# A state-space mixer's convolution, pace and sums, written in another way

## The chip, the cores and the metric

The kernel runs on one core of a Trainium2 chip. A core has engines that work side by side, each through its own row of instructions, in order: TensorE (PE) for matrix products, with the loading of weights (PEld) beside it; VectorE (DVE), ScalarE (ACT) and GpSimd (POOL) for everything else; SyncE (SP), which here only issues transfers (DMAs). Products are collected in PSUM, everything else lies in SBUF. The metric is the device time of one execution in microseconds (us). A profiled execution gives a trace of every instruction, with a clock granted to PE, where 1.00 is full speed.

## What is computed

One layer of a hybrid block on x of 1024 positions by 1024 channels, in float32. Two mixers read the same normalised input; each is mapped back to 1024 channels, gated and merged; a gated feed-forward layer follows. The change is in the second mixer, Mamba-2:

```python
def mamba2_mixer(z, xbc, dt, conv_w, conv_b, dt_bias, a_log, d_skip, w_norm):
    xbc = jax.nn.silu(causal_dwconv(xbc, conv_w, conv_b))      # 4 taps along the sequence
    xs, bm, cm = ...            # x: 4 groups x 8 heads x 64; B and C: 4 groups x 128
    delta = jax.nn.softplus(dt + dt_bias); a = -jnp.exp(a_log) * delta; xdt = xs * delta
    def step(state, inp):       # over chunks
        acum = jnp.cumsum(ac, axis=1)
        decay = jnp.exp(jnp.where(mask, acum_t - acum_s, -jnp.inf))
        y = einsum(C.B, decay, x) + einsum(C, state) * jnp.exp(acum)
        state = state * jnp.exp(a_last) + einsum(B, jnp.exp(a_last - acum), x)
        return state, y
    y = y + xs * d_skip
    y = y * jax.nn.silu(z)
    return rms_norm(y per group of 512 channels) * w_norm
...
merged = jax.nn.sigmoid(gate_a) * y_a + jax.nn.sigmoid(gate_b) * y_b
```

## The kernel before

**Dense products.** A projection has a block of 128 output channels as its unit (`Dense.unit`, L85): its weights (128x1024) are loaded, cast on ACT to a high part (`wh`, L75), and the low part is the difference (`wl`, L76, on GpSimd in this stage). For each half of the sequence (512 positions) 8 slices of the input are multiplied three times, low by high, high by low, high by high (L81, L82, L83): 24 products of 128x128 by 128x512 into one PSUM tile `dps` of a pool `psd` with three tiles. Then `evac` takes the tile away. With `fine=True` a unit yields after every three products, else only after each half.

**The fill.** `Fill.to(n)` draws steps of such units until n are done, so that dense products stand in PE's row between the smaller products of a recurrence. What is written between two calls of `fill.to` is the order in which instructions are issued; within it a scheduler may still set one engine's instructions some places apart, so PE's row is not quite the program's. The program's stages follow each other: front projections, the HGRN recurrence (up to about 828 us of the trace, with dense units, and the gate units GA7, GB0 and GB1, as its fill), `mamba_phase` (to about 1343 us), the branch products `dqs` whose operands `yr` are loaded from `ya_d` and `yb_d` (L946), and the feed-forward layer.

**The state-space stage.** It runs over 4 groups of 8 chunks of 128 positions. A group's six blocks (four of x, then B, then C) are units of the fill. Their `evac` (L797) copies the PSUM tile to `xp` in SBUF (L798), makes the fourth tap on ACT out of PSUM (L800), the other three on DVE out of `xp` at shifted columns (L802), and then Silu with `act`. `act` (L131) also loads ACT's table (L135) where the function belongs to another set than the last one: Exp and Ln share a set, Sigmoid and Silu have one each; the operation itself then has line L137.

For each chunk, `prepare` (L811) loads the decay rows `ac` and `eb`, makes them on ACT (L827, L137), transposes x (`trx`, L831), multiplies C by B (`cb`, L833), masks it (`cm`, L835), scales x twice (`xd`, `kx`, L837, L841), transposes B into the second half of the same PSUM tile (`cb`, L842), copies it out (`bt`, L844) and multiplies decay and `cm` (L845). `mix` (L850) has the products `yi` (within the chunk, L861), `yx` (from the state `Sm`, L867) and `sps` (into the state, L874), and adds them to x on DVE (last: L881). `finish` (L883) works on half a group, 512 positions: GpSimd multiplies z on (L890), ACT squares, DVE adds the four squares, `col_sums` splits the sum in two parts (`csh` on ACT, `csl` on DVE, L192) and PE sums over channels with two products into `smm` (L199, L200); Ln, Exp and a product (L901) norm the rows, and they are stored to `yb_d` (L902).

The order: 12 half units, `prepare(0, 0)`, then in every chunk the `prepare` of the next one, `finish` of the previous group's halves in chunks F0 = 1 and F1 = 4, the chunk's share of the fill at once (1.5 half units, or 5/8 of one in the last group), and `mix`. The last group's two `finish` calls stand after its last `mix`, then the LATE = 7 half units that are left.

Of the kernel before, what the change touches and what calls it, by code (L numbers as in the profile page):

```python
# [17 lines left out]
F0, F1 = 1, 4  # L18
LATE = 7
NGB = 2  # L20
# [101 lines left out]
def hybrid_block(ctx, tc, x, w_mod, w_ada, w_blk, w_i, w_ba, w_bb, w_o, w_g, w_u, w_d,  # L122
# [117 lines left out]
    def gate_evac(which, n):  # L240
        dst = (ga_d, gb_d)[which]

        def evac(th, ps):
            sg = wp.tile([P, TH], F32, tag="ge", name="ge")
            act(sg, ps, AF.Sigmoid)
            nc.sync.dma_start(out=dst[n, :, TH * th:TH * th + TH], in_=sg)
        return evac

    def gate_units(which, n0, n1, fine=False):
        for n in range(n0, n1):  # L250
            yield from dn.unit(w_blk[(B_GA, B_GB)[which] + n], uh, ul, gate_evac(which, n), fine=fine)
# [530 lines left out]
    def mamba_phase():  # L782
        with tc.tile_pool(name="m", bufs=2, reuse_waits="tile") as mp, \
                tc.tile_pool(name="mps", bufs=1, space=PSUM, reuse_waits="tile") as pp:
            grp, pre, state = {}, {}, {}

            def dense_x(g):
                xT = mp.tile([P, 4, T], F32, tag="xT", name="xTm", bufs=3)
                bT = mp.tile([P, T], F32, tag="bT", name="bT")
                cT = mp.tile([P, T], F32, tag="cT", name="cT")  # L790
                grp[g] = (xT, bT, cT)
                for blk, dst in [(4 * g + j, xT[:, j, :]) for j in range(4)] + [(16 + g, bT), (20 + g, cT)]:
                    xp = mp.tile([P, T + 3], F32, tag="xp", name="xp")
                    V.memset(xp[:, 0:3], 0.0)
                    cw = lambda j: cl[:, C_CW + 4 * blk + j:C_CW + 4 * blk + j + 1]

                    def evac(th, ps, xp=xp, dst=dst, cw=cw):  # L797
                        S.copy(xp[:, 3 + TH * th:3 + TH * th + TH], ps)  # L798
                        d = dst[:, TH * th:TH * th + TH]
                        S.activation(d, ps, AF.Identity, scale=cw(3))  # L800
                        for j in (2, 1, 0):
                            V.scalar_tensor_tensor(d, xp[:, TH * th + j:TH * th + j + TH], cw(j), d,  # L802
                                                   op0=ALU.mult, op1=ALU.add)
# [7 lines left out]
            def prepare(g, ch):  # L811
                xT, bT, cT = grp[g][:3]
                hs = slice(HG * g, HG * g + HG)
                cs = slice(P * ch, P * ch + P)
                h64 = lambda ap: ap.rearrange("p (h q) -> p h q", h=HG)
                ac = mp.tile([P, HG, P], F32, tag="ac", name="ac", bufs=2)
                nc.sync.dma_start(out=ac, in_=ac_d[ch, hs, :][None].broadcast_to([P, HG, P]))
                eb = None
                if ch:
                    eb = mp.tile([P, 4, P], F32, tag="eb", name="eb")  # L820
                    a2 = ac_d[ch, hs, :].rearrange("(j e) t -> e j t", e=2)
                    for e in range(2):
                        nc.sync.dma_start(out=eb[64 * e:64 * e + 64], in_=a2[e][None].broadcast_to([64, 4, P]))
                    act(eb, eb, AF.Exp)
                for h in range(HG):
                    n = HG * g + h
                    S.activation(ac[:, h, :], ac[:, h, :], AF.Relu, bias=acum[:, ch, n:n + 1], scale=-1.0)  # L827
                act(ac, ac, AF.Exp, scale=-1.0)
                tr = pp.tile([P, TH], F32, tag="tr", name="trx")
                for j in range(4):  # L830
                    PE.transpose(out=tr[:, P * j:P * j + P], in_=xT[:, j, cs], identity=ident)  # L831
                cb = pp.tile([P, TH], F32, tag="cb", name="cb")
                PE.matmul(cb[:, 0:P], bT[:, cs], cT[:, cs], start=True, stop=True)  # L833
                cm = mp.tile([P, P], F32, tag="cm", name="cm")
                V.tensor_tensor(cm, cb[:, 0:P], triu, op=ALU.mult)  # L835
                xd = mp.tile([P, TH], F32, tag="xd", name="xd")
                V.tensor_tensor(h64(xd), h64(tr), delta[:, ch, hs][:, :, None].broadcast_to([P, HG, HP]), op=ALU.mult)  # L837
                kx = bt = None
                if ch < TT - 1:
                    kx = mp.tile([P, TH], F32, tag="kx", name="kx")  # L840
                    V.tensor_tensor(h64(kx), h64(tr), wdec[:, ch, hs][:, :, None].broadcast_to([P, HG, HP]), op=ALU.mult)  # L841
                    PE.transpose(out=cb[:, P:2 * P], in_=bT[:, cs], identity=ident)  # L842
                    bt = mp.tile([P, P], F32, tag="bt", name="bt")
                    V.tensor_copy(bt, cb[:, P:2 * P])  # L844
# [3 lines left out]
                pre[g, ch] = (ac, eb, xd, kx, bt)  # L848

            def mix(g, ch):  # L850
                xT, bT, cT = grp[g][:3]
                hs = slice(HG * g, HG * g + HG)
                cs = slice(P * ch, P * ch + P)
                h64 = lambda ap: ap.rearrange("p (h q) -> p h q", h=HG)
                ac, eb, xd, kx, bt = pre.pop((g, ch))
                st = state.get(g)
                yi = pp.tile([P, 4, P], F32, tag="yi", name="yi")
# [5 lines left out]
                y = mp.tile([P, 4, P], F32, tag="yt", name="yt")  # L863
                if ch:
                    yx = pp.tile([P, 4, P], F32, tag="yx", name="yx")
                    for j in range(4):
                        PE.matmul(yx[:, j, :], st[:, P * j:P * j + P], cT[:, cs], start=True, stop=True)  # L867
                    V.tensor_tensor(y, yx, eb, op=ALU.mult)
                    V.tensor_tensor(y, y, yi, op=ALU.add)
                else:  # L870
                    V.tensor_copy(y, yi)
                if ch < TT - 1:
                    sps = pp.tile([P, TH], F32, tag="st", name="sps")
                    PE.matmul(sps, bt, kx, start=True, stop=True)  # L874
                    sn = state[g] = mp.tile([P, TH], F32, tag="S", name="Sm")
                    if ch:
                        V.tensor_tensor(h64(sn), h64(st), eal[:, ch, hs][:, :, None].broadcast_to([P, HG, HP]), op=ALU.mult)
                        V.tensor_tensor(sn, sn, sps, op=ALU.add)
                    else:
                        V.tensor_copy(sn, sps)  # L880
                V.tensor_tensor(xT[:, :, cs], xT[:, :, cs], y, op=ALU.add)  # L881

            def finish(g, hf):  # L883
                xT = grp[g][0]
                sl = slice(TH * hf, TH * hf + TH)
                sqs = mp.tile([P, TH], F32, tag="S", name="sqs")
                for j in range(4):
                    zs = mp.tile([P, TH], F32, tag="zs", name="zs", bufs=2)
                    nc.sync.dma_start(out=zs, in_=z_d[4 * g + j, :, sl])
                    G.tensor_tensor(xT[:, j, sl], xT[:, j, sl], zs, op=ALU.mult)  # L890
                    sq = sqs if j == 0 else mp.tile([P, TH], F32, tag="yt", name="sq")
# [3 lines left out]
                sm = pp.tile([P, TH], F32, tag="cb", name="smm")  # L895
                col_sums(sm, sqs, mp, ("yt", "yt"), V)
# [7 lines left out]
            fill = Fill(chain(*[dense_x(g) for g in range(GB)], gate_units(1, NGB, 8)))  # L904
            fill.to(12)
            prepare(0, 0)
            at = [12]
            for g in range(GB):
                n = 12 if g < GB - 1 else 16 - 2 * NGB - LATE
                at += [at[8 * g] + n * (c + 1) / 8 for c in range(TT)]  # L910
            for i in range(TT * GB):
                g, ch = divmod(i, TT)
                if i + 1 < TT * GB:
                    prepare(*divmod(i + 1, TT))
                if g and ch == F0:
                    finish(g - 1, 0)
                if g and ch == F1:
                    finish(g - 1, 1)
                fill.to(at[i + 1])
                mix(g, ch)  # L920
                if g == GB - 1 and ch == 7:
                    finish(g, 0)
                if g == GB - 1 and ch == 7:
                    finish(g, 1)
# [432 lines left out]
```

## Time and profile before

| | |
|---|---|
| runs, us | 2398.66, 2406.07, 2404.76 |
| median | 2404.76 |
| profiled execution | 2397.53, of which the span of the trace is 2395.7 |
| mean granted PE clock | 0.98 |
| state-space stage in the trace | about 828 to 1343 us |

Times in the trace are counted from the span's start. In a row of it, `PE L83 MATMUL dps<-uh,wh` is the instruction of line 83 on PE that writes `dps` from `uh` and `wh`; "L842 <- DVE cm L835" is idle time of PE ahead of its line 842 that DVE's `cm` of line 835 ended.

### The profile page before, as it was taken

What the parts mean: (1) busy time and instruction counts of PE and PEld (TensorE: products, weight loads), DVE (VectorE), ACT (ScalarE), POOL (GpSimd) and SP (SyncE); (2) the same over time, 40 slices, a digit from 0 to 9 for tenths busy, and PEclk for the clock granted to TensorE, in tenths of its full rate; (3) what the DMA queues carried; (4) which work ended last, traced back from release to release, by engine and by line L of the source; (5) the groups of instructions that cost most, each with busy time, mean ns of one, the idle gap of its engine ahead of it and who ended that gap; (6) DMA issues with size and microseconds to landing.
All of it is one profiled execution on the core that took longest, in us unless ns stands there. A gap on an engine that the chain in (4) does not pass through costs nothing.

```text
span 2395.7 us, 32127 instructions
## 1 busy us (share of the span) xinstructions
PE 2256.0 (94%) x12412; PEld 1824.6 (76%) x12412; DVE 1611.3 (67%) x2452; ACT 1096.7 (46%) x1894; POOL 393.8 (16%) x239
## 2 busy tenths in 40 slices
PE   7799999999999998989897999999999999999996
PEld 4578888877777786767675788888778888888785
DVE  6967655548788467787878434458887666655657
ACT  4533333046666658778787411223533333322232
POOL 0600000012222222222213000003410000013224
PEclk9999999999999999999999999999999999999999
DMA  7344325611111222333444734433233222244544
GB/s 272 103 148 132 128 90 194 196 40 54 59 54 54 93 67 93 122 108 118 135 126 158 254 129 154 135 102 129 76 122 106 92 71 88 78 151 145 167 150 152
DMA packets 116032, 290.23 MB, mean 121 GB/s; under 512 B 12324, under 2 KB 27172, under 8 KB 115880
## 3 DMA queue, kind: packets, MB, share of 16 engines
q1 hardware_dynamic: 115880, 288.19, 36.2%
q8 instruction: 97, 1.59, 0.3%
q14 instruction: 55, 0.45, 0.1%
HBM read 234.52 MB, written 53.62 MB: 120 GB/s over the span
## 4 chain that ended last, share of the span: by engine, by line
PE 65%; DVE 14%; ACT 7%; DMA 4%; issue 3%; POOL 2%; POOLq 0%; DVEq 0%; SPq 0%; ACTq 0%
PE fps L81 8%; PE fps L82 8%; PE fps L83 8%; PE dps L81 8%; PE dps L82 8%; PE dps L83 8%; PE dqs L81 4%; PE dqs L82 4%; PE dqs L83 4%; DVE xTm L802 2%; DMA ac<-ac_d 1%; PE hps L83 1%; PE hps L81 1%; PE hps L82 1%; ACT ac L827 1%
## 5 line engine op out<-in xcount | busy, mean ns | idle before, releaser
L81 PE MATMUL dps<-uh,wl 128*128 128x512 f32 x800 | 330.4, 413 | 7.3 <-POOL wl L76 3.8
L82 PE MATMUL dps<-ul,wh 128*128 128x512 f32 x800 | 320.9, 401 | 0.0
L83 PE MATMUL dps<-uh,wh 128*128 128x512 f32 x800 | 320.8, 401 | 0.0
L75 ACT CAST wh<-raw 128x1024 fp32r<-128x1024 f32 x113 | 118.4, 1049 | 266.9 <-PE fps L83 147.4
L76 POOL TENSOR_TENSOR wl<-raw,wh 128x1024 fp32r<-128x1024 f32 x50 | 131.8, 2638 | 552.0 <-ACT wh L75 460.8
L81 PEld LDWEIGHTS dps<-uh,wl 128*128 128x128 f32 x800 | 156.2, 195 | 38.2 <-issue 6.0
L83 PEld LDWEIGHTS dps<-uh,wh 128*128 128x128 f32 x800 | 153.7, 192 | 32.9 <-issue 0.8
L82 PEld LDWEIGHTS dps<-ul,wh 128*128 128x128 f32 x800 | 154.4, 193 | 29.6 <-issue 1.3
L1225 POOL TENSOR_TENSOR wdr<-wdr,rws 128x512 f32<-128x512 f32 x44 | 70.8, 1612 | 529.9 <-DMA rws<-g_d 368.7
L81 PE MATMUL dqs<-yp,wl 128*128 128x512 f32 x384 | 149.3, 390 | 1.1 <-ACT yp L191 1.1
L82 PE MATMUL dqs<-yp,wh 128*128 128x512 f32 x384 | 149.5, 390 | 0.0
L83 PE MATMUL dqs<-yp,wh 128*128 128x512 f32 x384 | 149.2, 389 | 0.0
L191 ACT CAST cw<-raw 128x512 fp32r<-128x512 f32 x131 | 80.7, 621 | 130.3 <-PE fps L83 87.1
L76 DVE TENSOR_TENSOR wl<-raw,wh 128x1024 fp32r<-128x1024 f32 x63 | 78.3, 1243 | 91.1 <-ACT wh L75 91.1
L81 PE MATMUL fps<-t,cw 128*128 128x512 f32 x352 | 137.0, 389 | 0.5 <-ACT p L1115 0.5
L82 PE MATMUL fps<-t,cw 128*128 128x512 f32 x352 | 136.9, 389 | 0.0
L83 PE MATMUL fps<-t,cw 128*128 128x512 f32 x352 | 136.9, 389 | 0.0
L81 PE MATMUL fps<-wd,wl 128*128 128x512 f32 x304 | 119.1, 392 | 3.1 <-DVE wl L76 3.1
L802 DVE SCALAR_TENSOR_TENSOR xTm<-xp,cl,xTm 128x512 f32<-128x512 f32 x96 | 101.9, 1072 | 27.7 <-ACT xTm L800 26.7
L82 PE MATMUL fps<-wd,wh 128*128 128x512 f32 x304 | 118.9, 391 | 0.0
L83 PE MATMUL fps<-wd,wh 128*128 128x512 f32 x304 | 118.7, 391 | 0.0
L192 DVE TENSOR_TENSOR cw<-raw,cw 128x512 fp32r<-128x512 f32 x109 | 79.7, 733 | 41.4 <-ACT cw L191 40.2
(364 smaller groups left out, 5635.1 us busy)
## 6 DMA issues: line engine op xcount, KB each, us to landing
raw<-in_w_blk_dram SPq DMA_DIRECT2D x78, 512.0 KB, 3.4
raw<-h_d SPq DMA_DIRECT2D x44, 512.0 KB, 3.5
wa<-in_w_ada_dram SPq DMA_DIRECT2D x32, 512.0 KB, 4.6
ac<-ac_d SPq DMA_DIRECT2D x32, 512.0 KB, 4.1
raw<-in_w_g_dram SPq DMA_DIRECT2D x26, 512.0 KB, 3.9
raw<-in_w_u_dram SPq DMA_DIRECT2D x26, 512.0 KB, 3.4
wdr<-in_w_d_dram SPq DMA_DIRECT2D x44, 256.0 KB, 3.1
h_d<-sg SPq DMA_DIRECT2D x18, 512.0 KB, 2.9
```

The costliest lines, as they stand in the source:

```text
L75: nc.scalar.copy(wh, raw)
L76: (eng or self.lo).tensor_tensor(wl, raw, wh.bitcast(F32), op=ALU.subtract)
L81: nc.tensor.matmul(ps, sl, mh, start=first, stop=False)
L82: nc.tensor.matmul(ps, sh, ml, start=False, stop=False)
L83: nc.tensor.matmul(ps, sh, mh, start=False, stop=last)
L191: S.copy(hi, src)
L192: eng.tensor_tensor(lo, src, hi.bitcast(F32), op=ALU.subtract)
L802: V.scalar_tensor_tensor(d, xp[:, TH * th + j:TH * th + j + TH], cw(j), d, op0=ALU.mult, op1=ALU.add)
L827: S.activation(ac[:, h, :], ac[:, h, :], AF.Relu, bias=acum[:, ch, n:n + 1], scale=-1.0)
L1225: G.tensor_tensor(raw, raw, g2r[:, halves[nh]], op=ALU.mult)
```

## The change

- **Convolution.** The copy to `xp` is gone. The three taps on DVE read the PSUM tile, each half by itself at 509 to 512 columns; six columns around the border between the halves are kept in a small tile `edge`, and the second half's first three columns get three small products more. Silu is applied after every second block, to both. B and C come first in a group, the x blocks behind them.
- **Fill.** All units in this stage yield after three products. A chunk's share (12 such steps; 6.5 in the last group) is drawn in two halves, one ahead of `mix` and one behind it, and LEAD = 12 steps more stand ahead of the first chunk; LATE is now 32 such steps.
- **Chunk.** `ac` is loaded two chunks ahead (three buffers), `eb` in `fetch_e`. Both `cb` products come right behind the transpositions. The product of decay and `cm` is a part of its own, `scores`, behind the `mix` before. `mix` has the order `yx`, `sps`, `yi`.
- **Sums.** `finish` is cut in `squares` (up to the split) in chunks 0 and 3 and `finish` (from the sums on) two chunks later; `smm` is a tile of `psd`. In the last group half 0 is squared in chunk 5, and half 1 after the last `mix`; eight steps of the fill stand ahead of the last `finish`.
- **Gates.** Gate units that run in fine steps, those in HGRN's fill too, have Exp, Ln, Exp for Sigmoid.

```diff
-F0, F1 = 1, 4
-LATE = 7
+F0, F1 = 0, 3
+LATE, LEAD = 32, 12
...
+            if logs:
+                act(sg, ps, AF.Exp, scale=-1.0)
+                act(sg, sg, AF.Ln, bias=ones[:, 0:1])
+                act(sg, sg, AF.Exp, scale=-1.0)
+            else:
+                act(sg, ps, AF.Sigmoid)
...
-                for blk, dst in [(4 * g + j, xT[:, j, :]) for j in range(4)] + [(16 + g, bT), (20 + g, cT)]:
-                    xp = mp.tile([P, T + 3], F32, tag="xp", name="xp")
-                    V.memset(xp[:, 0:3], 0.0)
+                held = []
+                for blk, dst in [(16 + g, bT), (20 + g, cT)] + [(4 * g + j, xT[:, j, :]) for j in range(4)]:
+                    held.append((blk, dst))
+                    edge = mp.tile([P, 6], F32, tag="edge", name="edge")
...
-                        S.copy(xp[:, 3 + TH * th:3 + TH * th + TH], ps)
                         d = dst[:, TH * th:TH * th + TH]
                         S.activation(d, ps, AF.Identity, scale=cw(3))
+                        if th:
+                            V.tensor_copy(edge[:, 3:6], ps[:, 0:3])
+                        else:
+                            V.tensor_copy(edge[:, 0:3], ps[:, TH - 3:TH])
                         for j in (2, 1, 0):
-                            V.scalar_tensor_tensor(d, xp[:, TH * th + j:TH * th + j + TH], cw(j), d,
+                            o = 3 if th else 3 - j
+                            V.scalar_tensor_tensor(d[:, o:], ps[:, o + j - 3:TH + j - 3], cw(j), d[:, o:],
                                                    op0=ALU.mult, op1=ALU.add)
-                        if blk >= 20:
-                            act(d, d, AF.Silu, bias=cl[:, C_CB + blk:C_CB + blk + 1])
-                        elif th:
-                            act(dst, dst, AF.Silu, bias=cl[:, C_CB + blk:C_CB + blk + 1])
-                    yield from dn.unit(w_blk[B_X + blk], uh, ul, evac)
+                            if th:
+                                V.scalar_tensor_tensor(d[:, 0:3], edge[:, j:j + 3], cw(j), d[:, 0:3],
+                                                       op0=ALU.mult, op1=ALU.add)
+                        if th and len(held) == 2:
+                            for k, t in held:
+                                act(t, t, AF.Silu, bias=cl[:, C_CB + k:C_CB + k + 1])
+                            held.clear()
+                    yield from dn.unit(w_blk[B_X + blk], uh, ul, evac, fine=True)
...
+                PE.matmul(cb[:, 0, :], bT[:, cs], cT[:, cs], start=True, stop=True)
+                if ch < TT - 1:
+                    PE.transpose(out=cb[:, 1, :], in_=bT[:, cs], identity=ident)
...
-                V.tensor_tensor(ac, ac, cm[:, None, :].broadcast_to([P, HG, P]), op=ALU.mult)
+            def scores(g, ch):
+                ac, cm = pre[g, ch][:2]
+                V.tensor_tensor(ac, ac, cm[:, None, :].broadcast_to([P, HG, P]), op=ALU.mult)
...
-            def finish(g, hf):
+            def squares(g, hf):
...
+                split(*hl, sqs, V)
+                fin[g, hf] = sqs, hl
+            def finish(g, hf):
...
+                sqs, (hi, lo) = fin.pop((g, hf))
+                sm = psd.tile([P, TH], F32, tag="d", name="smm")
+                PE.matmul(sm, ones_r, lo, start=True, stop=False)
+                PE.matmul(sm, ones_r, hi, start=False, stop=True)
...
             for i in range(N):
                 g, ch = divmod(i, TT)
+                if i + 2 < N:
+                    fetch(*divmod(i + 2, TT))
                 if i + 1 < N:
                     prepare(*divmod(i + 1, TT))
...
+                if g:
+                    for f, hf in ((F0, 0), (F1, 1)):
+                        if ch == f:
+                            squares(g - 1, hf)
+                        if ch == f + 2:
+                            finish(g - 1, hf)
...
+                fill.to((share(i) + share(i + 1)) / 2)
                 mix(g, ch)
...
+                if i + 2 < N:
+                    fetch_e(*divmod(i + 2, TT))
+                if i + 1 < N:
+                    scores(*divmod(i + 1, TT))
+                if g == GB - 1 and ch == 5:
+                    squares(g, 0)
+                fill.to(share(i + 1))
+            finish(g, 0)
+            squares(g, 1)
+            fill.to(total + 8)
+            finish(g, 1)
             fill.drain()
```

**PE, a chunk of the second group in which sums are made**, before (`dps` are the dense products, `uh` and `ul` the two parts of the input, `mk` the identity; the lone `cb` transposition of L842 stands at another place of the chunk, behind dense products):

```order
L83 MATMUL dps<-uh_93,wh 128x512
L861 MATMUL yi<-ac,xd 64x128 x8
L867 MATMUL yx<-cT,Sm 128x128 x4
L874 MATMUL sps<-kx,bt 128x512
L199 MATMUL smm<-csl,ones_r 128x512
L200 MATMUL smm<-csh,ones_r 128x512
L831 MATMUL trx<-mk,xTm 128x128 x4
L81 MATMUL dps<-uh_92,wl 128x512
L82 MATMUL dps<-ul_94,wh 128x512
L833 MATMUL cb<-cT,bT 128x128
L83 MATMUL dps<-uh_92,wh 128x512
```

and with the change, first at `prepare` and the sums, and 18 dense products later at `mix`:

```order
L83 MATMUL dps<-uh_92,wh 128x512
L850 MATMUL trx<-mk,xTm 128x128 x4
L852 MATMUL cb<-cT,bT 128x128
L854 MATMUL cb<-mk,bT 128x128
L936 MATMUL smm<-csl,ones_r 128x512
L937 MATMUL smm<-csh,ones_r 128x512
L81 MATMUL dps<-uh_92,wl 128x512
```

The rows of `mix`:

```order
L83 MATMUL dps<-uh_93,wh 128x512
L889 MATMUL yx<-cT,Sm 128x128 x4
L892 MATMUL sps<-kx,bt 128x512
L897 MATMUL yi<-ac,xd 64x128 x8
L81 MATMUL dps<-uh_93,wl 128x512
```

The sums stood right behind the mix whose group's half they close; now they stand behind `prepare`, with both `cb` products ahead of them, and there are dense products between `prepare` and `mix` and behind `mix`.

**ACT, at the end of the HGRN stage**, before (`sc` and `oT` belong to HGRN's last chunks, `ge` is a gate, `csh` the high part of a split sum, `wh` a weight's):

```order
L682 COPY sc<-sc_ps_3616 128x128
L719 ACTIVATE sq<-oT 128x512
L191 CAST csh<-sq 128x512
L137 ACTIVATE ge<-dps 128x512
L135 ACT_TABLE_LOAD
L137 ACTIVATE sq<-sum,kc 128x512
L75 CAST wh<-raw 128x1024
L137 ACTIVATE sq<-sq 128x512
L135 ACT_TABLE_LOAD
```

and with the change:

```order
L724 ACTIVATE sq<-oT 128x512
L191 CAST csh<-sq 128x512
L137 ACTIVATE ge<-dps 128x512
L75 CAST wh<-raw 128x1024
L137 ACTIVATE ge<-ge,mk 128x512
L137 ACTIVATE ge<-ge 128x512
L137 ACTIVATE sq<-sum,kc 128x512
L137 ACTIVATE sq<-sq 128x512
L135 ACT_TABLE_LOAD
L806 ACTIVATE bT<-dps,cl 128x512
```

The table load between the gate and `sum` is gone, two operations on `ge` are added, and the cast of the gate's weight stands ahead of the two operations on `sum`.

**SP, from the last loads of z to the first operand of the branch products**, before (`raw` is a weight of the branch products, `gb_d` the gates' store):

```order
L889 DMA zs<-z_d 128x512 x2
L902 DMA yb_d<-xTm 128x512 x4
L70 DMA raw<-in_w_ba_dram 128x1024
L902 DMA yb_d<-xTm 128x512 x4
L246 DMA gb_d<-ge 128x512 x2
L946 DMA yr<-ya_d 128x1024
```

and with the change:

```order
L943 DMA yb_d<-xTm 128x512 x4
L251 DMA gb_d<-ge 128x512
L922 DMA zs<-z_d 128x512
L943 DMA yb_d<-xTm 128x512 x4
L1008 DMA yr<-ya_d 128x1024 x2
```

The load `yr` stands behind the last stores to `yb_d` in both; between the stores of half 0 and those of half 1 there is now a load of z.

More of the change, by code (lines that the diff above doesn't have):

```diff
@@ L250, in gate_units @@
         for n in range(n0, n1):
-            yield from dn.unit(w_blk[(B_GA, B_GB)[which] + n], uh, ul, gate_evac(which, n), fine=fine)
+            yield from dn.unit(w_blk[(B_GA, B_GB)[which] + n], uh, ul, gate_evac(which, n, fine), fine=fine)
     def combo(pool, tag, src, eng=V, **k):
@@ L823, in prepare @@
                         nc.sync.dma_start(out=eb[64 * e:64 * e + 64], in_=a2[e][None].broadcast_to([64, 4, P]))
-                    act(eb, eb, AF.Exp)
+                    dec[g, ch, 1] = eb
+            h64 = lambda ap: ap.rearrange("p (h q) -> p h q", h=HG)
+            def prepare(g, ch):
+                xT, bT, cT = grp[g]
+                hs = slice(HG * g, HG * g + HG)
+                cs = slice(P * ch, P * ch + P)
+                tr = pp.tile([P, TH], F32, tag="tr", name="trx")
+                for j in range(4):
+                    PE.transpose(out=tr[:, P * j:P * j + P], in_=xT[:, j, cs], identity=ident)
+                cb = pp.tile([P, 2, P], F32, tag="cb", name="cb")
+                PE.matmul(cb[:, 0, :], bT[:, cs], cT[:, cs], start=True, stop=True)
+                if ch < TT - 1:
+                    PE.transpose(out=cb[:, 1, :], in_=bT[:, cs], identity=ident)
+                ac, eb = dec.pop((g, ch)), dec.pop((g, ch, 1), None)
                 for h in range(HG):
@@ L828, in prepare @@
                 act(ac, ac, AF.Exp, scale=-1.0)
[L829 to L833, printed above, removed]
+                if ch:
+                    act(eb, eb, AF.Exp)
                 cm = mp.tile([P, P], F32, tag="cm", name="cm")
-                V.tensor_tensor(cm, cb[:, 0:P], triu, op=ALU.mult)
+                V.tensor_tensor(cm, cb[:, 0, :], triu, op=ALU.mult)
                 xd = mp.tile([P, TH], F32, tag="xd", name="xd")
@@ L862, in mix @@
                                   start=True, stop=True)
[L863 removed]
+                y = mp.tile([P, 4, P], F32, tag="yt", bufs=1, name="yt")
                 if ch:
[L865 to L867 removed]
                     V.tensor_tensor(y, yx, eb, op=ALU.mult)
[L869 to L871 removed]
                 if ch < TT - 1:
[L873 to L874 removed]
                     sn = state[g] = mp.tile([P, TH], F32, tag="S", name="Sm")
@@ L880, in mix @@
                         V.tensor_copy(sn, sps)
+                if ch:
+                    V.tensor_tensor(y, y, yi, op=ALU.add)
+                else:
+                    V.tensor_copy(y, yi)
                 V.tensor_tensor(xT[:, :, cs], xT[:, :, cs], y, op=ALU.add)
-            def finish(g, hf):
+            def squares(g, hf):
                 xT = grp[g][0]
                 sl = slice(TH * hf, TH * hf + TH)
-                sqs = mp.tile([P, TH], F32, tag="S", name="sqs")
+                sqs = mp.tile([P, TH], F32, tag="sqs", name="sqs", bufs=1)
+                hl = [mp.tile([P, TH], F32R, tag="hl", name=n) for n in ("csh", "csl")]
                 for j in range(4):
@@ L902, in finish, with share @@
                     nc.sync.dma_start(out=yb_d[4 * g + j, :, sl], in_=xT[:, j, sl])
-            fill = Fill(chain(*[dense_x(g) for g in range(GB)], gate_units(1, NGB, 8)))
-            fill.to(12)
-            prepare(0, 0)
[L907 to L911, printed above, removed]
+            N = TT * GB
+            fill = Fill(chain(*[dense_x(g) for g in range(GB)], gate_units(1, NGB, 8, True)))
+            total = 96 * GB + 16 * (8 - NGB) - LATE
+            fetch(0, 0)
+            fill.to(96 + LEAD)
+            fetch(0, 1)
+            fetch_e(0, 1)
+            prepare(0, 0)
+            scores(0, 0)
+            def share(i):
+                if i <= N - TT:
+                    return 96 + LEAD + 12 * i
+                a = 96 + LEAD + 12 * (N - TT)
+                return a + (total - a) * (i - N + TT) / TT
+            for i in range(N):
                 g, ch = divmod(i, TT)
-                if i + 1 < TT * GB:
+                if i + 2 < N:
+                    fetch(*divmod(i + 2, TT))
+                if i + 1 < N:
                     prepare(*divmod(i + 1, TT))
[L915 to L919, printed above, removed]
-                mix(g, ch)
[L921 to L924, printed above, removed]
+                if g:
[5 more added lines that the diff above has]
+                fill.to((share(i) + share(i + 1)) / 2)
+                mix(g, ch)
+                if i + 2 < N:
+                    fetch_e(*divmod(i + 2, TT))
+                if i + 1 < N:
+                    scores(*divmod(i + 1, TT))
[6 more added lines that the diff above has]
+            finish(g, 1)
             fill.drain()
```

41 lines of the change are left out of this document (22 added, 19 removed).

## The prediction

> **What bounds the kernel now.** I read the page's busy times first, then its stretches by stage, then PE's waits in the state-space stage, then single rows. The two rows of the page:
>
> ```profile
> span 2395.7 us, 32127 instructions
> PE 2256.0 (94%) x12412; PEld 1824.6 (76%) x12412; DVE 1611.3 (67%) x2452; ACT 1096.7 (46%) x1894; POOL 393.8 (16%) x239
> ```
>
> PE is busy 94% of the span, so a change pays where PE stands, runs at a lower clock, or gets fewer products; it gets the same number here. The stretches of the stage (columns: stretch, its length, then busy us and instructions of PE, PEld, DVE, ACT, POOL, then PE's granted clock, DMA share and GB/s) are the lead into the first group, groups 0 to 3, and the tail:
>
> ```profile
> 828.00:893.00 65.00, 65.00 (x288) 53.81 (x287) 35.21 (x38) 31.41 (x54) 17.71 (x7) 1.00 0.29 88
> 893.00:1002.00 109.00, 99.78 (x569) 77.57 (x568) 87.24 (x124) 86.70 (x167) 21.41 (x11) 1.00 0.28 94
> 1002.00:1114.00 112.00, 100.53 (x551) 78.36 (x550) 89.58 (x135) 89.94 (x177) 27.71 (x15) 0.95 0.37 121
> 1114.00:1227.00 113.00, 99.39 (x545) 77.14 (x544) 91.74 (x132) 89.57 (x175) 27.48 (x15) 0.95 0.36 119
> 1227.00:1300.00 73.00, 66.90 (x406) 50.67 (x405) 59.42 (x87) 64.51 (x128) 21.98 (x12) 1.00 0.53 167
> 1300.00:1343.00 43.00, 29.56 (x119) 23.17 (x118) 20.40 (x21) 18.08 (x25) 8.29 (x5) 0.84 0.59 193
> ```
>
> In the lead PE does nothing but projection products without a gap: 65.0/288 = **0.226 us per product**. In groups 0 to 2 it stands 9 to 14 us, and its clock falls to 0.95; DVE and ACT are 80% busy beside it. PE's waits over the stage (total, times, longest) are
>
> ```profile
> PE smm L199 <- DVE csl L192: 23.9, 6, 8.8
> PE cb L842 <- DVE cm L835: 17.0, 10, 4.1
> PE cb L833 <- ACT cT L137: 5.0, 3, 1.7
> PE dps L81 <- ACT ge L137: 3.4, 1, 3.4
> ```
>
> The first two make 41 us, and both are waits of PE's order: the sum of squares stands in PE's row before its split is made, and the second `cb` product shares a PSUM tile with the first, which DVE has yet to read (`cm`).
>
> **What PE needs per chunk.** Starts of rows in PE's timeline of one chunk, and the lone `cb` transposition (min/median/max ns):
>
> ```profile
> 916.88 0.39 PE L83 MATMUL dps<-uh,wh 128*128 128x512 f32 x1
> ...
> 920.66 0.47 PE L81 MATMUL dps<-uh,wl 128*128 128x512 f32 x1
> L842 PE MATMUL cb<-mk,bT x28: 270/328/383, 894.7 to 1282.6; 128*128 128x128 f32 x28
> ```
>
> From the last product's end (916.88 + 0.226) to the next product is 3.55 us for `yi`, `yx`, `sps`, `trx` and one `cb`; with 0.33 for the other `cb` a chunk's small products cost 3.88. The new order gives a chunk of groups 0 to 2 36 dense products: 36 x 0.226 + 3.88 = **12.0 us**.
>
> The last DVE row of chunk (0,0), and of chunk 7 of each group:
>
> ```profile
> 912.82 0.68 DVE L881 TENSOR_TENSOR xTm<-xTm,yt 128x512 f32<-128x512 f32 x1
> 1001.43 0.69 DVE L881 TENSOR_TENSOR xTm<-xTm,yt 128x512 f32<-128x512 f32 x1
> 1112.92 0.68 DVE L881 TENSOR_TENSOR xTm<-xTm,yt 128x512 f32<-128x512 f32 x1
> 1226.19 0.68 DVE L881 TENSOR_TENSOR xTm<-xTm,yt 128x512 f32<-128x512 f32 x1
> 1299.26 0.69 DVE L881 TENSOR_TENSOR xTm<-xTm,yt 128x512 f32<-128x512 f32 x1
> ```
>
> So 828 to chunk (0,0) takes 84.8, the other 23 chunks of groups 0 to 2 take 88.6 + 111.5 + 113.3 = 313.4, group 3 73.1.
>
> **Groups 0 to 2.** PE's need is 23 x 12.0 + 1.8 (four pairs of sums, 2 x 0.226 each) = 277.8. The two waits go by order: `cb` is complete before `cm` asks for it, and the sums stand two chunks behind their split, so 24 us of PE work cover them. What is late next is the last x block at a group's start: its dense products end right at the next group's transpositions, and `trx` of that block waits for ACT's fourth tap, DVE's three and the Silu. I put 2.5 us on each of three boundaries, 7.5 (0 to 15). For other waits on DVE or ACT, in a row that still holds many engines in order, I allow 5 (0 to 17). Sum 277.8 + 7.5 + 5 = 290.3, against 313.4: **-23** (-35 to -3).
>
> Whether DVE lets PE run so depends on the taps. Rows of DVE (busy, mean ns; then idle before), two tile views, and two small operations:
>
> ```profile
> L802 DVE SCALAR_TENSOR_TENSOR xTm<-xp,cl,xTm 128x512 f32<-128x512 f32 x96 | 101.9, 1072 | 27.7 <-ACT xTm L800 26.7
> L802 DVE SCALAR_TENSOR_TENSOR bT<-xp,cl,bT 128x512 f32<-128x512 f32 x24 | 22.0, 916 | 5.6 <-ACT bT L800 5.3
> L802 DVE SCALAR_TENSOR_TENSOR cT<-xp,cl,cT 128x512 f32<-128x512 f32 x24 | 20.1, 836 | 8.8 <-ACT cT L800 8.7
> L802 DVE SCALAR_TENSOR_TENSOR xTm<-xp,cl,xTm x96: 733/747/2930, 834.7 to 1192.4; 128x512 f32<-128x512 f32 x96
> L721 DVE SCALAR_TENSOR_TENSOR y<-oT,cl,gs x16: 735/750/752, 539.0 to 825.8; 128x512 f32<-128x512 f32 x16
> L308 DVE TENSOR_TENSOR modc<-mps,cl 128x2 f32<-128x2 f32 x8 | 1.3, 161 | 4.9 <-PE mps L307 4.7
> L181 DVE SCALAR_TENSOR_TENSOR mv<-mv 128x1 f32<-128x1 f32 x8 | 2.3, 291 | 3.0 <-POOL mv L179 2.8
> ```
>
> A tap out of SBUF takes 747 ns at the median and up to 2930; the nearest operation with one input in PSUM (L721) takes 735 to 752, never more. The excess over 0.745 on the three tap rows is 31.4 + 4.1 + 2.2 = 37.7 us, 9.4 per group. I take it as gone, since the new taps have L721's form; kept, it is 0. Added are per block two copies and three products of 3 columns, 30 a group; between 0 and 0.291 each, I take the nearest by size and place, 0.161: 4.8 (0 to 8.7). DVE in groups 1 and 2 is then 90.7 (mean of 89.58 and 91.74) - 9.4 + 4.8 = 86 of the 96 us that PE needs.
>
> [...]
>
> For ACT the rows are
>
> ```profile
> L798 ACT COPY xp<-dps 128x512 f32<-128x512 f32 x48 | 27.5, 572 | 13.9 <-PE dps L83 13.8
> L135 ACT ACT_TABLE_LOAD x50 | 64.2, 1283 | 0.7
> L137 ACT ACTIVATE ge<-dps 128x512 f32<-128x512 f32 x11 | 6.5, 597 | 6.6 <-DMA gb_d<-ge 3.4 <-PE dps L83 3.2
> 803.14 1.28 ACT L135 ACT_TABLE_LOAD   x1
> 804.43 0.60 ACT L137 ACTIVATE ge<-dps 128x512 f32<-128x512 f32 x1
> ```
>
> It loses 48 copies (27.5 us) and, by its new order, all but about 20 of these 50 table loads (30 x 1.283 = 38 us); each of the 12 gate evacuations gets two operations more (24 x 0.6 = 14). A group's ACT falls from 89.8 to about 74. ACT also waits for the decay rows of `ac`:
>
> ```profile
> ACT ac L827 <- DMA ac<-ac_d: 30.6, 19, 5.5
> ```
>
> Their loads are now issued two chunks ahead on SP, ahead of the z loads of the squares; the scores that need them have a chunk of PE work in front of their mix, and the squares two in front of their sums. So I count this wait, and what ACT is freed of, at nothing beyond the allowance; if that cover were gone, the 30.6 would bound it. [...]
>
> **First chunk and HGRN's end.** 342 products now lie ahead of the first mix: 342 x 0.226 + 3.9 = 81.2 against 84.8 with 324; I leave 1.6 of waits: **-2** (-4 to +2). Ahead of the stage the last gate weight's cast now precedes the sums' casts on ACT, so its low half is ready:
>
> ```profile
> 808.92 0.80 PE L81 MATMUL dps<-uh,wl 128*128 128x512 f32 x1 [3.19 <-POOL wl L76]
> 807.50:814.30 6.80, 5.38 (x13) 4.22 (x14) 3.32 (x7) 2.15 (x3) 3.74 (x2) 0.50 0.48 158
> ```
>
> The 3.2 us stall goes, and with it part of the half clock behind it (0.50 over 6.8 us, some 2): **-5** (-6 to 0).
>
> **Group 3 and the tail.** Group 3 now gets 164 products up to its last mix (before: 120): 164 x 0.226 + 8 x 3.88 = 68, plus 2 for waits: 70 against 73.1, **-3** (-7 to +4). For the tail:
>
> ```profile
> 1314.70 0.79 PE L199 MATMUL smm<-csl,ones_r 128*128 128x512 f32 x1 [8.80 <-DVE csl L192]
> 1319.36 0.77 PE L81 MATMUL dps<-uh,wl 128*128 128x512 f32 x1 [3.44 <-ACT ge L137]
> 1321.58 0.42 SPq L946 DMA_DIRECT2D yr<-ya_d  x1
> 1342.92 0.39 PE L81 MATMUL dqs<-yp,wl 128*128 128x512 f32 x1
> ```
>
> The last mix to `smm` is 15.4 us, to the first operand load 22.3, to the branch products 43.7. Half 0 is now squared two chunks earlier and only half 1 is left, so I put `smm` at 13 (the loads of z for its last block stand on SP behind half 0's stores). The load still stands behind the `yb_d` stores, 6.9 later, and the operand chain from load to product was 21.3 with 104 dense products beside it; 72 (16.3 us) no longer cover it, so PE waits at its end. With 19 for the chain: 39 against 43.7, **-5** (-9 to +3).
>
> **Sum.** -5 - 2 - 23 - 3 - 5 = -38. The profiled execution took 2397.53 us (span 2395.7 and 1.8 around it), which gives 2360; the median of the runs, 2404.76, stands 7.2 above it, so I put **2367**.
>
> **Rivals.** *DVE becomes the bound.* The taps keep their excess (their other input and their output are in SBUF, and GpSimd runs 27.7 us of a group) and the edges cost 0.291: DVE has 90.7 + 8.7 = 99.4 in a group, and with some 4 of waits 103.5, against 98.5 in my sum. That is +5 in each of groups 0 to 2, and 2 at the boundary of group 3: 2384. For it: the tap rows' maxima. Against: L721's. Chance 0.17.
> *PE fully covered.* Boundaries and allowance are 0, group 3 is 68, the tail gets its 9, the rest as forecast: -5 - 4 - 35 - 5 - 9 = -58, 2347. For it: PE's lead alone runs gapless with DVE at 54%. Against: no group does. Chance 0.12.
> *The in-order pair DVE and ACT sets the pace, and gets worse.* A half's taps now hold one of three PSUM tiles of the dense products, and the sums use that pool too. If DVE keeps its idle time (112 - 89.6 = 22.4 a group, most of it waits for ACT) on top of 99.4, a group takes 121.8, against 111.5 and 113.3: +9 in each of groups 0 to 2, 27, less HGRN's 5 and the tail's 5: +17, 2422. It decides from the point where DVE's busy time and waits exceed 111 us a group. Against it: a half is 24 products and 2/3 of a chunk, 8 us, so a tile is asked for only 16 us after its last product. Chance 0.08.
> *No change: the stalls only move.* PE gives up `smm` and `cb`, and waits the same time for `sps` or a dense tile instead; HGRN's 5 is left, 2400. Against: each of these has a chunk, 12 us, of cover now. Chance 0.08.
>
> **How the numbers follow.** The forecast has 0.55, from 2355 to 2380 by its own bounds. 0.3% (7.2 us) is about what a measurement of this kernel can tell from no change. Faster by more: 0.55 + 0.17 + 0.12 = 0.84; within: 0.08; slower: 0.08. The range takes in the covered case and the DVE case with its bounds, 2346 to 2392, and leaves the last two out.
>
> **What would show it.** Right: PE's rows `smm` and `cb` without waits; chunks of groups 0 to 2 at 12 to 12.6 us; taps at 730 to 760 ns; PE's clock at 1.00 there; a wait of `trx` for the last x block at three boundaries; PE idle some 9 us ahead of `dqs`. Wrong: taps over 0.8 us, edge rows over 0.2, `dps` waiting for DVE inside a group, or a tail over 44 us.

## The result and the profile after

| | before | after |
|---|---|---|
| median of the runs, us | 2402.86 (4 runs, 2398.66 to 2406.07) | 2364.78 (4 runs, 2363.22 to 2367.86) |
| ratio, 95% interval | | 0.9844 (0.9824 to 0.9864) |
| profiled execution | 2397.53 | 2364.60 |
| its span | 2395.7 | 2362.8 |

The kernel got 38 us faster by the runs and 33 by the two profiled executions; 2367 was predicted. In the later comparisons the kernel before had medians of 2397.3 to 2400.0; against those it is 33 to 35. The page's two rows of the kernel after:

```profile
span 2362.8 us, 32206 instructions
PE 2248.6 (95%) x12412; PEld 1825.3 (77%) x12412; DVE 1599.0 (68%) x2548; ACT 1043.6 (44%) x1839; POOL 391.4 (17%) x239
```

PE does the same 12412 products in 7 us less busy time, and its time without a product fell from 139.7 us (2395.7 - 2256.0) to 114.2. The view by stretches shows the groups, cut where the last DVE row of their chunk 7 ends (columns as before: length, then busy us of PE, PEld, DVE, ACT, POOL, clock, DMA share, GB/s):

```profile
910.00:995.30 85.30, 82.11 (x476) 65.49 (x475) 70.56 (x128) 60.90 (x127) 18.75 (x9) 1.00 0.34 105
995.30:1098.50 103.20, 96.05 (x540) 76.30 (x539) 91.15 (x156) 74.51 (x154) 26.42 (x14) 0.95 0.43 131
1098.50:1200.60 102.10, 97.73 (x547) 77.66 (x546) 92.18 (x157) 75.95 (x155) 25.91 (x14) 0.97 0.41 132
1200.60:1272.70 72.10, 68.08 (x414) 52.76 (x414) 56.09 (x86) 55.91 (x128) 19.97 (x11) 0.97 0.54 170
```

Groups 0 to 2 take 85.3 + 103.2 + 102.1 = 290.6 us, for 313.4 before; group 3 72.1 for 73.1. ACT fell from 89.8 to 75 a group; DVE did **not** fall. PE's waits in the stage:

```profile
PE trx L850 <- ACT xTm L137: 14.7, 3, 7.2
PE smm L936 <- DVE csl L192: 12.9, 1, 12.9
PE yi L897 <- ACT csh L191: 2.3, 1, 2.3
PE yx L889 <- DVE Sm L906: 1.8, 2, 1.4
PE trx L850 <- DVE kx L869: 1.4, 1, 1.4
```

Nothing of `cb` is left, and one wait of `smm`, in the tail. In its place three waits of `trx` stand, one at each group boundary. The longest sum on ACT's own list is its wait for the decay rows `ac`. That row, and rows of ACT ahead of the longest wait of `trx`, which ended at 1093.70:

```profile
ACT ac L858 <- DMA ac<-ac_d: 31.1, 15, 6.3
1087.25 0.98 ACT L858 ACTIVATE ac<-ac,acum 128x128 f32<-128x128 f32 x3 [2.80 <-DMA ac<-ac_d]
1088.14 0.67 ACT L806 ACTIVATE xTm<-dps,cl 128x512 f32<-128x512 f32 x1
1091.55 1.04 ACT L75 CAST wh<-raw 128x1024 fp32r<-128x1024 f32 x1
1092.50 1.15 ACT L137 ACTIVATE xTm<-xTm,cl 128x1024 f32<-128x1024 f32 x1
```

At all three boundaries ACT waited for a load of `ac` (6.3, 2.8 and 1.4 us) just ahead of the last x block's fourth tap (L806), and cast a weight between that block's taps and its Silu (L137). Rows of DVE in the stage, and two tile views (min/median/max ns):

```profile
L813 DVE SCALAR_TENSOR_TENSOR xTm<-dps,cl,xTm 128x509 f32<-128x509 f32 x64 | 47.3, 739 | 0.1
L816 DVE SCALAR_TENSOR_TENSOR xTm<-edge,cl,xTm 128x3 f32<-128x3 f32 x48 | 28.8, 600 | 0.0
L816 DVE SCALAR_TENSOR_TENSOR cT<-edge,cl,cT 128x3 f32<-128x3 f32 x12 | 9.3, 774 | 0.0
L816 DVE SCALAR_TENSOR_TENSOR bT<-edge,cl,bT 128x3 f32<-128x3 f32 x12 | 4.2, 352 | 0.0
L813 DVE SCALAR_TENSOR_TENSOR xTm<-dps,cl,xTm x96: 729/740/751, 852.0 to 1192.6; 128x509 f32<-128x509 f32 x64, 128x511 f32<-128x511 f32 x16, 128x510 f32<-128x510 f32 x16
L816 DVE SCALAR_TENSOR_TENSOR xTm<-edge,cl,xTm x48: 203/214/2409, 857.3 to 1193.2; 128x3 f32<-128x3 f32 x48
```

The taps out of PSUM take 740 ns and never more than 751. The three-column products take 0.21 us at the median, but 42.3 in all 72, 0.59 on average: 27 us over the median stand there, for 37.7 on the taps before.

The tail's rows (the last z load, its multiply, the last sums, the first operand load, the first branch product):

```profile
1284.38 0.62 SPq L922 DMA_DIRECT2D zs<-z_d  x1
1288.98 1.26 POOL L923 TENSOR_TENSOR xTm<-xTm,zs 128x512 f32<-128x512 f32 x1 [8.56 <-DMA zs<-z_d]
1293.07 0.79 PE L936 MATMUL smm<-csl,ones_r 128*128 128x512 f32 x1 [12.90 <-DVE csl L192]
1298.97 0.90 SPq L1008 DMA_DIRECT2D yr<-ya_d  x2
1311.62 0.39 PE L81 MATMUL dqs<-yp,wl 128*128 128x512 f32 x1
```

The last mix's row starts at 1272.0, so the tail takes 39.6 us, for 43.7 before; but `smm` comes later than before, 21.1 us behind it instead of 15.4. Behind the last sums PE has 72 dense products without a gap up to the first branch product.

### The profile page after: what moved, and what is told of

Same layout as the page of the kernel before. It is cut to its first block, busy times and chain, and to the rows that moved or that the text cites. A ratio compares the mean times of both kernels' runs of the same rounds, so it can differ in the third digit from the quotient of the medians.

```text
span 2362.8 us, 32206 instructions
## 1 busy us (share of the span) xinstructions
PE 2248.6 (95%) x12412; PEld 1825.3 (77%) x12412; DVE 1599.0 (68%) x2548; ACT 1043.6 (44%) x1839; POOL 391.4 (17%) x239
## 4 chain that ended last, share of the span: by engine, by line
PE 68%; DVE 14%; ACT 6%; DMA 4%; POOL 2%; issue 1%; SPq 0%; POOLq 0%; DVEq 0%; ACTq 0%
PE dps L81 8%; PE dps L83 8%; PE dps L82 8%; PE fps L81 8%; PE fps L82 8%; PE fps L83 8%; PE dqs L81 4%; PE dqs L83 4%; PE dqs L82 4%; DVE eb L657 1%; PE hps L83 1%; PE hps L81 1%; PE hps L82 1%; DVE xTm L813 1%; DVE e L649 1%
## 5 line engine op out<-in xcount | busy, mean ns | idle before, releaser
L179 POOL TENSOR_TENSOR mv<-mv,kc 128x1 f32<-128x1 f32 x32 | 28.5, 898 | 419.2 <-DVE mv L178 410.7
```

The costliest lines, as they stand in the source:

```text
L179: G.tensor_tensor(mv[:, 2:3], mv[:, 1:2], kc[:, 2:3], op=ALU.pow)
```

## Experiments

Two theories stood behind the prediction. **A**: PE sets the pace, and the change puts its row in an order in which it no longer waits. **B**: DVE and ACT set it, and PE's waits only tell that they are late. Ratios are to the kernel before, run beside each kernel on its chip (its median there 2397.3 to 2400.0); the change has 0.9844 (0.9824 to 0.9864). A trace is one execution: e9 below changes only the tail, and its groups 0 to 2 take 295.0 us for the change's 290.6, so differences of some 5 us in the groups of one trace are not read.

**Sums at once** (e1): one part of the order undone.

```diff
                         if ch == f:
                             squares(g - 1, hf)
-                        if ch == f + 2:
                             finish(g - 1, hf)
```

> The changed kernel with finish right behind squares in the same chunk for groups 0 to 2. Theory A (PE sets the pace, and the sums' two chunks of distance took PE's wait for csl away): PE waits for csl again at six places, 2 to 4 us each, so +10 to +20 us on the changed kernel's 2365: 2375 to 2385. Theory B (DVE and ACT set the pace of a group, and PE's waits only tell of it): within 3 us of 2365.

0.9834 (0.9812 to 0.9856), 2360.5 us: no loss. PE's waits for `smm` became three, 18.3 us, of which 13.4 are the tail's, and the boundary waits fell to 9.3. So the distance of two chunks isn't what took the waits for `csl` out of the groups (15.1 us before: 23.9 less the tail's 8.8).

**The B transposition behind again** (e2).

```diff
-                if ch < TT - 1:
-                    PE.transpose(out=cb[:, 1, :], in_=bT[:, cs], identity=ident)
...
+                    PE.transpose(out=cb[:, 1, :], in_=bT[:, cs], identity=ident)
                     bt = mp.tile([P, P], F32, tag="bt", name="bt")
```

> The changed kernel with the transposition of B asked for behind kx again, as before; in PE's row it then stands 3 to 6 dense products behind the first cb product. Theory A: PE waits for DVE's cm again at some of 28 places, 10 to 17 us in all: 2375 to 2382. Theory B: within 3 us of 2365. A third way, that 3 to 6 dense products (0.7 to 1.4 us) cover most of it because cm is quick: +3 to +6.

0.9872 (0.9848 to 0.9895), 2367.9: not clear of the change. Its waits of PE:

```profile
PE cb L868 <- DVE cm L861: 14.6, 15, 2.2
PE smm L935 <- DVE csl L192: 14.2, 1, 14.2
PE trx L850 <- ACT xTm L137: 5.7, 3, 2.8
```

The waits for `cm` are back with 14.6 us, and those at the boundaries are 9 us shorter; that DVE and ACT catch up while PE waits in the chunks is a reading of this, not shown. Groups 0 to 2 take 297.5 us, only 2.5 more than in e9, and the 3 us of time lie at the edge of theory B and of the third way.

**Sigmoid gates** (e4): `gate_evac(which, n)` for `gate_evac(which, n, fine)`.

> The changed kernel with Sigmoid gates and their table loads again. Theory A: the stall at HGRN's end comes back (3 to 6 us) and the rest hides: 2368 to 2372. Rival: the loads, some 40 more at 1.28 us each, also hold up dense tiles in group 3, where a gate unit stands in each chunk: +10 or more, 2375 and up.

0.9891 (0.9871 to 0.9911), 2374.2: clearly slower than the change. The stall at HGRN's end is back in the same form:

```profile
810.33 0.80 PE L81 MATMUL dps<-uh,wl 128*128 128x512 f32 x1 [3.20 <-POOL wl L76]
```

The first mix then ends 7.3 us later from HGRN's start than in the change. The whole is 9.4 us by the medians and 11 by the ratios, near the rival's number but not at its place: group 3 is only 1.6 us longer. So most of it lies at HGRN's end, and more there than theory A's 3 to 6.

**Taps alone** (b1): the kernel before with the taps and edges of the change and nothing else of it.

```diff
-                        S.copy(xp[:, 3 + TH * th:3 + TH * th + TH], ps)
...
-                            V.scalar_tensor_tensor(d, xp[:, TH * th + j:TH * th + j + TH], cw(j), d,
+                            o = 3 if th else 3 - j
+                            V.scalar_tensor_tensor(d[:, o:], ps[:, o + j - 3:TH + j - 3], cw(j), d[:, o:],
```

> The kernel before with only the three taps read out of PSUM, edges as in the change, order of blocks and Silu as before. Theory A (order of PE's row made the gain): PE still waits for csl and cm, so -6 to +3 us on before. Theory C (the convolution made it): -15 us or more. In both the 3-column products should show the waiting for GpSimd that the taps showed: about 0.6 us on average, near 0.21 at the median.

0.9928 (0.9910 to 0.9946), 2382.5: 17 us, theory C's number, and a surprise. By its trace groups 0 to 2 take 295.7 us for 313.4, and PE's waits shrink, although neither the sums nor the transposition were moved in the program:

```profile
PE smm L199 <- DVE csl L192: 13.1, 5, 4.2
PE cb L848 <- DVE cm L841: 11.6, 9, 2.1
```

**Taps, and the copy kept on ACT** (b2): b1 with the `S.copy` to `xp`, which nothing reads.

> The kernel before with the taps out of PSUM (which alone took 17 us off), and the copy to xp kept on ACT although nothing reads it. If ACT's time made that gain (its busy time fell by 6 us a group, DVE's did not), it goes back to within 5 us of before. If it was the form of the taps, it stays at -13 us or lower. Between, both have a part.

0.9907 (0.9888 to 0.9927), 2376.8: the gain stays, so ACT's 27.5 us of copies were not the cause. Groups 0 to 2 take 291.1 us, as few as in the whole change. Groups 1 and 2 of its trace:

```profile
1010.90:1111.80 100.90, 96.14 (x547) 75.22 (x546) 88.78 (x158) 89.77 (x175) 27.79 (x14) 1.00 0.40 134
1111.80:1213.10 101.30, 97.71 (x546) 76.21 (x544) 89.21 (x158) 89.85 (x175) 27.75 (x14) 0.98 0.39 133
```

DVE and ACT are as busy here as before (89.6 and 89.9 us in group 1, which then took 112), so their busy time does not explain the gain.

**The transposition ahead, alone** (b3): the kernel before with L842's transposition directly behind L833.

> The kernel before with only the transposition of B moved directly behind the first cb product; taps out of SBUF, sums and fill as before. In the kernels with the taps alone the scheduler also moved that transposition up to 8 dense products further back, so they do not tell taps from order. If PE's order is the cause, the 17 us of cb waits go and 8 to 15 us of the time with them: 2385 to 2392. If the waits only show that DVE is late, PE waits elsewhere: within 4 us of before.

0.9985 (0.9971 to 0.9998), 2393.7: 4 us. The 17 us of waits for `cm` went, and PE waited elsewhere (`smm` 23.9 before, `cT` 5.0, `yi` 1.8):

```profile
PE smm L199 <- DVE csl L192: 30.3, 8, 7.1
PE cb L833 <- ACT cT L137: 6.8, 3, 3.7
PE yi L862 <- DVE yt L870: 4.0, 2, 2.8
```

This is what B says of a wait that is removed by order alone.

**Taps out of SBUF in the changed kernel** (e11): the converse of b1, with PE's row almost untouched.

```diff
+                        xp = mp.tile([P, TH + 3], F32, tag="xp", name="xp")
+                        S.copy(xp[:, 3:], ps)
...
-                            V.scalar_tensor_tensor(d[:, o:], ps[:, o + j - 3:TH + j - 3], cw(j), d[:, o:],
+                            V.scalar_tensor_tensor(d, xp[:, j:j + TH], cw(j), d,
                                                    op0=ALU.mult, op1=ALU.add)
```

> The changed kernel with the taps out of SBUF again: each half is copied on ACT to a half-long xp with its three border columns, two buffers; the split's two parts lie in the z tiles to make room. PE's row is that of the change but for five places around group boundaries, so this tells the taps' form from the order of PE's row, which the kernels with the taps alone did not. If the form made the gain of groups 1 and 2 (18 of the 23 us there with taps alone): they go back to 108 to 113 us each, +12 us or more in all. If the order did: groups within 2 us of the change, 0 to +5 in all, although DVE's taps wait for GpSimd again (mean over 1 us) and ACT has 27 us more.

0.9912 (0.9897 to 0.9927), 2378.3: 13.5 us lost by the medians, 16 by the ratios. Its groups 0 to 2, its waits, and one tap row:

```profile
914.70:1002.10 87.40, 81.92 (x466) 65.47 (x465) 70.79 (x112) 65.28 (x137) 17.02 (x8) 0.98 0.29 93
1002.10:1110.80 108.70, 98.24 (x547) 77.24 (x546) 98.24 (x138) 81.57 (x168) 30.36 (x15) 0.95 0.40 124
1110.80:1216.70 105.90, 98.08 (x547) 77.17 (x546) 97.29 (x138) 81.42 (x168) 27.82 (x14) 0.97 0.39 128
```

```profile
PE trx L849 <- ACT xTm L137: 20.2, 3, 7.9
PE yx L888 <- DVE Sm L905: 6.1, 3, 3.3
```

```profile
L815 DVE SCALAR_TENSOR_TENSOR cT<-xp,cl,cT 128x512 f32<-128x512 f32 x24 | 26.0, 1084 | 5.6 <-ACT cT L808 5.2
```

302.0 us for 290.6: by the two profiled executions (2375.6 and 2364.6) the whole loss is in these groups. Group 1 goes back to the 108 to 113 that was expected, group 2 not quite. DVE now has 97 to 98 us of work where PE needs 97 (8 x 12.0, and 0.9 for two pairs of sums), and 91 to 92 in the change; that this is why PE loses time is argued, not shown. ACT has its copies back too (81.5 us for 75), and this run alone doesn't tell them from the taps; b2 does so in the old order, where the copies stayed and the gain too.

**No border products** (e8): the three `L816` products left out.

> The changed kernel without the three 3-column products at the border of the halves (the first three positions of the second half lack their earlier taps). They take 42 us of DVE over the stage, 0.21 us at the median. Theory: the excess over 0.21 is waiting for GpSimd that the next operation with two inputs in SBUF takes over, so DVE loses only some 15 us, and the time 0 to 4. Rival: they are a cost of their own: DVE loses 35 us or more and the time 8 or more.

0.9841 (0.9822 to 0.9861), 2361.4: no clear gain. From 828 us to the last mix DVE is busy 331.9 us for 362.1, 30 less, although 42.3 us of operations are gone: some 12 turn up in others. That is nearer the rival's 35 than the theory's 15, so the products are in good part a cost of their own to DVE; the time did what the theory said. With DVE at 85 instead of 91 to 92 us in groups 1 and 2, groups 0 to 2 take 288.6, no clear difference from 290.6.

**The z loads on GpSimd's queue** (e5): `G.dma_start` for `nc.sync.dma_start` in `squares`.

> The changed kernel with the loads of z issued from GpSimd's queue, so that neither their wait for a buffer nor the stores ahead of them on SP hold up others. Theory: SP's order makes two of the waits that are left. Then ACT's wait for ac falls from 31 to under 15 us, PE's wait for trx from 14.7 to under 9, for the last smm from 12.9 to under 5, and the time by 10 to 15 us. Rival: only the tail is SP's, the boundary is ACT's own order (taps, cast, Silu): -9 or less, ac and trx waits as they are. A third: issuing costs GpSimd time and delays the weights' low halves: 0 or slower.

0.9901 (0.9882 to 0.9919), 2375.5: clearly slower than the change. The theory falls:

```profile
PE trx L850 <- ACT xTm L137: 18.4, 3, 7.7
PE smm L936 <- DVE csl L192: 13.2, 1, 13.2
ACT ac L858 <- DMA ac<-ac_d: 24.0, 13, 5.9
```

ACT still waits 24 us for `ac`, so SP's z loads make at most 7 of its 31.1. Issuing the 32 loads takes 18.2 us of GpSimd (0.57 each); the time is the third way's, but PE's list shows no wait for a weight's low half, so its reason isn't shown.

**The last z loads first** (e9), in the tail; **LEAD = 18** (e10), one line; and **both with e1** (e12).

```diff
+            zs = zloads(g, 1)
             finish(g, 0)
-            squares(g, 1)
+            squares(g, 1, zs)
```

> The changed kernel with the last four loads of z issued ahead of half 0's last finish, two of them into idle ac tiles. Theory: smm's wait of 12.9 us falls to 3 to 5, and 72 products behind it still cover the operand chain: -8 to -10 us. Rival: the operand chain behind the yb_d stores is the bound, and PE waits at dqs instead: 0 to -3.

> The changed kernel with LEAD = 18: the last x block of a group is complete 18 products (4.1 us) before the next group's transpositions. Theory: the three waits of trx, 14.7 us in all with the longest 7.2, are the chain of taps and Silu behind the last block, and the cover comes off each: trx waits under 5 us, time 6 to 10 us less, 2353 to 2357. Rival: the wait moves to the next late thing (yx, yi) in the same chunk: 0 to 3 us.

> The changed kernel with finish right behind squares, LEAD = 18 and the last z loads ahead of half 0's finish. Each took 0 to 4 us off some stage of its own profile, none a clear amount off the time. If they add, 2350 to 2356; if PE's waits only change their place, 2358 to 2364.

e9: 0.9868 (0.9848 to 0.9888), 2368.5, no gain. The wait for the last `smm` fell to 8.3 and the tail to 36.0 us, 3.6 less, where 8 to 10 were expected: GpSimd's four products now run in one piece and end at 1280.5, but the tile `sqs` has one buffer and half 0's norm holds it, so the first square of half 1 comes late and `smm` 4 us behind it:

```profile
1287.03 0.63 ACT L935 ACTIVATE sqs<-xTm 128x512 f32<-128x512 f32 x1 [2.68 <-DVE xTm L952]
...
1291.27 0.79 PE L946 MATMUL smm<-csl,ones_r 128*128 128x512 f32 x1 [8.30 <-DVE csl L192]
```

e10: 0.9849 (0.9828 to 0.9870), 2362.6: `trx` still waits 11.5 us with 4.1 more of cover ahead of each, and DVE begins to hold dense tiles (2.2 us): the rival's size, if not its place. e12: 0.9872 (0.9856 to 0.9889), 2366.3: group 3 (66.5) and the tail (33.7) have their small gains, and the time hasn't; it lies above both ranges. No version here is clearly faster than the change.

## Why the prediction was right, and where its steps were not

The time from the HGRN recurrence's first product to the branch products is 824.4 us before and 791.9 after. Term by term, measured on the two profiled executions (chunk ends and first products; for the first row the 36 dense products that now stand ahead of the first transposition are taken off at 0.226 us), against the prediction:

| term | predicted | measured |
|---|---|---|
| HGRN's end and the first chunk | -5, -2 | -6.0, +1.3 |
| groups 0 to 2 | -23 | -22.8 |
| group 3 | -3 | -1.0 |
| tail | -5 | -4.1 |
| outside these | 0 | -0.4 |
| sum | -38 | -33 |

Each term was within 3.3 us of its size and the largest within 0.2, but with a scatter of some 5 us between traces that is partly luck. So is the last step: the sum gave 2360 for the profiled execution, which took 2364.6, and the 7.2 us that were added for the median of the runs made up for it; after the change the median (2364.78) does not stand above the profiled execution. And several steps failed:

- **"The two waits go by order"** came true of the waits in the groups (of the 23.9 us of `smm`, 8.8 were the tail's and stayed there), but failed as a cause. Moving the transposition alone gave 4 us of time for 17 of waits, putting it back cost 3, not clear of the change, and putting the sums back cost nothing. What carries the most is the taps' form: of the 22.8 us in the groups it alone gives 17.7 (b1) or 22.3 (b2), and without it, in the changed order, 11.4 are lost. The two overlap, since the change without it (e11) keeps the other 11.4.
- **"I take the excess as gone"** (9.4 us of DVE a group) failed. L721's form was the right row for a tap (740 to 751 ns at median and most), but much of the excess went on to the border products, which at 0.59 us on average were over the 0.2 that was named as a sign of being wrong. The two copies a block took the 0.16 us that was put on all five operations; the three products a block, 18 a group, were mis-sized, 0.59 for 0.16, which is 7.7 us more. DVE has 91 to 92 us a group, between the forecast's 86 and the 99.4 of the rival "DVE becomes the bound", and no dense tile waits for DVE in PE's list. The run without these products shows that there is no clear time to gain from them.
- **ACT's wait for `ac`, counted at nothing** because its loads are issued two chunks ahead, is 31.1 us for 30.6 before. The cover was not there: from the fourth on, these loads were issued only 3.9 to 9.8 us ahead of the rows that read them, less than one chunk (the load read at 1087.25 was issued at 1081.88 and landed at 1087.16). The wait now stands ahead of the last x block's fourth tap at each boundary. No run here removes it, so how much of the boundaries is due to it, or to the weight's cast behind it, stays open.
- **The boundaries** were taken at 2.5 us each and cost 4.9 (3 waits, 14.7), within the bounds of 0 to 15; of the 5 for other waits only 1.4 came in groups 0 to 2. The groups' sum, 290.3, held with 290.6.
- **What ACT is freed of, counted at nothing**, was right for the copies (b2). The gates' table loads were priced only as HGRN's stall, -5; bringing them back cost 9 to 11 us, 7.3 of them ahead of the first mix.
- **The tail** is right in sum and wrong in both halves. `smm` was put at 13 us and comes at 21.1: the last z load, issued at 1284.4 behind half 0's stores, ends GpSimd's wait of 8.6. I had named this load and not priced it. And the operand chain (21.3 before, put at 19) was never what PE waited for: the first operand was split by 1306.0, and PE came to `dqs` at 1311.6, at the end of its 72 dense products. Before it was the same: split by 1329.6, and `dqs` at 1342.9 behind dense products without a gap (the trace has 96 behind the last sums, not 104). So the 21.3 was the length of PE's own row, and fewer dense products behind `smm` made the second half short.
- **PE's clock** was expected at 1.00 in groups 1 and 2 and stayed at 0.95 and 0.97. The view by stretches gives 0.50 from 1088.4 to 1098.6 and from 1194.2 to 1201.0, during and after the two longer pauses at boundaries (7.2 and 4.4 us), and 1.00 around the first (3.2 us).

**What stays open**: by which way the taps' form gains 17 us and more in the old order, with the busy time of DVE, and in b2 of ACT too, unchanged. There the scheduler also set the transposition of B later (behind the first `cb` product in chunks 5 and 6 of group 1: 21 and 24 dense products before, 29 and 27 with taps alone), so form and order aren't apart in b1 and b2; only e11 nearly keeps PE's row. That b3's order alone gives 4 us, with all waits for `cm` gone, speaks for the form, but isn't the same move.

## What to carry to other kernels

A wait that ends last on the busiest engine names who was late, not what the wait is worth: remove one alone, or put one back alone, before pricing it, since an engine that is late can show up at the next thing that is asked of it (in b3 the 17.0 us of waits for `cm` went, and the rows of `smm`, `cT` and `yi` grew from 30.7 to 41.1). Nor does a helper engine's busy time tell the pace by itself: DVE at 85 or 92 us a group made no clear difference in the changed order and 98, with the taps out of SBUF again, came with 11 us more over three groups, but in the old order a group with DVE at 89 us took 112 in one form of the taps and 101 in the other. And in a tail, the load that stands behind a store on one queue (here it ended a wait of 8.6 us) has to be priced like any other operation on the path, and before a chain of operands is priced, look whether they were ready long before the product that reads them.

## What the runs showed of the hardware

The two traces have operations of DVE with both tensor inputs in SBUF that lasted until a GpSimd instruction ended, or about 0.55 us longer, at 3 columns as at 512. Of the 72 three-column products in the kernel after, the 52 that lay beside no GpSimd instruction took 203 to 219 ns. The 20 others took 31.3 us together; 17 of them ended within 0.03 us behind the GpSimd instruction that they overlapped, and the longest, 2.41 us, lay beside a weight subtraction of 2.39 us. Of the 144 taps out of SBUF in the kernel before, 21 took 1.65 to 2.93 us, and each of them ended 0.55 to 0.56 us behind the end of a GpSimd instruction that it overlapped; the 123 others took 733 to 755 ns. Of the 144 taps with one input in PSUM in the kernel after, 50 overlapped a GpSimd instruction and none took more than 751 ns. By which way an operation is held up, no trace here shows.
